# A two-layer decoder trunk in fp32 on one core: norms with 32 partitions per head, memory tiles ahead of the first query tile, and the inverses' recursion kept in program order

## The chip, the cores and the metric

The kernel runs on one core of one Trainium2 chip. The metric is the device time of one execution in microseconds. The engines are named as in the profile: PE is the matmul engine (PEld its weight loads), DVE the vector engine, ACT the scalar engine, POOL the GpSimd engine, SP the engine that issues most of the DMAs.

## The reference

One sequence of 256 tokens with 2048 channels passes through two layers. Each has one wide input projection, a token mixer, cross attention of four heads into 256 memory tokens, a gate silu(z), an output projection and a layer norm. The mixer of the first layer is a chunkwise retention, that of the second a gated delta rule. The change lies in the second layer:

```python
def gdn_branch(x, w_in, conv_w, a_log, dt_bias, norm_g):
    h = x @ w_in
    qkv = causal_conv_silu(h[..., :CONV_CH], conv_w)      # conv of width 4, then silu
    q = q * lax.rsqrt(jnp.sum(jnp.square(q), -1, keepdims=True) + NORM_EPS)
    k = k * lax.rsqrt(jnp.sum(jnp.square(k), -1, keepdims=True) + NORM_EPS)
    ...
    o = gated_delta_rule(q, k, v, g, beta)

def gated_delta_rule(q, k, v, g, beta):
    lower = jnp.where(strict, jnp.einsum('bhnid,bhnjd->bhnij', k_beta, kc) * decay, 0.0)
    a_mat = lower + jnp.eye(CHUNK, dtype=jnp.float32)
    u = lax.linalg.triangular_solve(a_mat, v_beta, left_side=True, lower=True, unit_diagonal=True)
    w = lax.linalg.triangular_solve(a_mat, k_beta * jnp.exp(g_cum)[..., None], left_side=True, lower=True, unit_diagonal=True)
    ...
```

There are 12 query and key heads of 128 channels and 24 value heads, so q and k are three tiles of four heads each (q0 to q2, k0 to k2).

## The kernel before, in words

**The weight stream.** All projections are split products: each fp32 weight is taken as a high and a low part, each activation too, and PE runs high by high, high by low and low by high. The weights come in units of 1024 numbers on each of 128 partitions (512 KB). SP issues a unit's DMA into one of four raw buffers; ACT rounds it to the high half (`split`, L173), DVE subtracts to get the low half (L174), and both go into rings of three. In the program's order a unit is loaded two units ahead of its use (`LOOK`). In the trace the units of the input projections are called `win_62` and the like, the halves `win_62h` and `win_62l`; for q, k and v tiles the matmuls with the high half are L303, those with the low half L310, and for z tiles both are L270.

**Order of the tiles.** `ORD1` lists the second layer's tiles: four tiles of the memory's keys and values (kv0 to kv3), the gates' columns (ab), the key tiles, the query tiles, two tiles of memory queries with their gates (mq, zm), and then the pairs v and z. The loop at the end of the function goes through this list; each tile's weights are streamed, and its result is handed to a generator.

**Work beside the stream.** The generators (`kq_tile`, `gdn_round`, `gdn_level`, `gdn_qc`, `gdn_pair` and others) are kept in `bg`. After every weight unit `bg.slot` lets them issue some work, by credits, in order of priority. So the stream is cut in many places by small groups of matmuls, and ACT, DVE and POOL run the generators' operations between the halves of the weights. The tile framework then settles the final order on each engine; an instruction in `tc.keep_in_program_order` stays behind everything that was traced before it on its engine.

**Norms of q and k** (`kq_tile`, L876 and following). After the conv (L864 to L871: an ACT copy, then three multiply-adds on DVE for each block of 128 channels, a tanh and a product) the squares of 128 channels have to be summed over the partitions. Two mults on POOL square the lower 64 partitions of two heads each (L886, 64x512), two ACT operations square the upper 64 (L887), POOL adds the two (L889, 128x512), and four matmuls (L895) with a selector of two columns sum over 64 partitions each.

**The inverses** (`gdn_gram`, `gdn_round`, `gdn_level`). The triangular matrices of four pairs of heads are inverted together: their blocks of 32 are copied to `LD` (L977, L979), transposed (L986), and a recursion of 31 steps on DVE, each a product (L993) and a subtraction (L995), gives the inverses of the blocks in `X`. Two transposes (L1002, L1004) follow, and `gdn_level` builds the inverses of 64 and 128 from them with small matmuls (named lv0 to lv5). `gdn_qc` makes the key and query products (`kq`, L1071 to L1073) and the weights `D` (L1078 to L1083).

Of the kernel before, what the change touches and what calls it, by code (L numbers as in the profile page):

```python
# [13 lines left out]
AF = mybir.ActivationFunctionType  # L14
ALU = mybir.AluOpType
AX = mybir.AxisListType

P = 128
# [20 lines left out]
PRM_NG, PRM_GG, PRM_CW, PRM_AL, PRM_DT, PRM_N = 0, 24, 25, 217, 218, 219  # L39
CST_ID, CST_U, CST_SU, CST_CAP, CST_IF, CST_SG, CST_SEL, CST_N = 0, 128, 256, 384, 512, 513, 514, 516  # L40

# [23 lines left out]
ORD0 = ["kv0", "kv1", "kv2", "kv3", "mq0", "zm0", "mq1", "zm1"]  # L65
ORD1 = ["kv0", "kv1", "kv2", "ab", "k0", "k1", "kv3", "q0", "mq0", "zm0", "mq1", "zm1", "k2", "q1", "q2"]
for _p in range(NPAIR):
# [59 lines left out]
def hybrid_kernel(ctx: ExitStack, tc: tile.TileContext, io: dict, stop=None):  # L127
    nc = tc.nc
# [11 lines left out]
    cst = cst_p.tile([P, CST_N], F32, name="cst")  # L140
# [4 lines left out]
    cap = cst[:, CST_CAP : CST_CAP + P]  # L145
    sel = cst[:, CST_SEL : CST_SEL + 2]
    mexp = cst_p.tile([P, 16], F32, name="mexp")
# [438 lines left out]
    for l, order, mem_ in ((0, ORD0, mem0), (1, ORD1, mem1)):  # L586
        j = 0
# [129 lines left out]
    for i, nm in enumerate(ORD0):  # L717
# [8 lines left out]
        p = int(nm[-1])  # L726
# [149 lines left out]
    def kq_tile(nm, ps):  # L876
        p = int(nm[1])
        lst, s0 = (kT, 8) if nm[0] == "k" else (qT, 9)
        lst[p] = stile(s0 + 2 * p, [P, 4, S], F32, nm + "T")
        src = lst[p]  # L880
        yield from conv(src, ps, (12 if nm[0] == "k" else 0) + 4 * p)
        fold = wtile("t2b", T2B, [P, 2, S], "fd" + nm)
        sq = wtile("t2", T2, [P, 2, S], "sq" + nm)
        for b in range(2):
            lo_, hi_ = src[0:64, 2 * b : 2 * b + 2, :], src[64:128, 2 * b : 2 * b + 2, :]
            nc.gpsimd.tensor_tensor(fold[64 * b : 64 * b + 64], lo_, lo_, op=ALU.mult)  # L886
            nc.scalar.activation(sq[64 * b : 64 * b + 64], hi_, AF.Square)  # L887
        yield 0.0
        nc.gpsimd.tensor_tensor(fold, fold, sq, op=ALU.add)  # L889
        yield 0.0  # L890
        yield 0.0
        pm = mx("n" + nm)
        for hh in range(2):
            for c in range(2):
                nc.tensor.matmul(pm[:, 4 * c + 2 * hh : 4 * c + 2 * hh + 2], fold[:, hh, c * P : c * P + P], sel, start=True, stop=True)  # L895
        hs = slice(4 * p, 4 * p + 4)
        pn = pm[:, 0:8].rearrange("p (c h b) -> p c b h", c=2, h=2)
        if nm[0] == "q":
# [63 lines left out]
    def gdn_round(rnd, wait, grams, s_ld, s_sl, s_x, wait2):  # L962
# [18 lines left out]
        SL = stile(s_sl, [P, 32, 32], F32, "SL%d" % rnd)  # L981
        X = stile(s_x, [P, 32, 32], F32, "X%d" % rnd)
# [7 lines left out]
        for j in range(31):  # L990
            n, m = 31 - j, j + 1
            t_ = tmp[:, 0 : n * m].rearrange("p (a b) -> p a b", b=m)
            nc.vector.tensor_tensor(t_, SL[:, j + 1 : 32, j : j + 1].broadcast_to([P, n, m]),  # L993
                                    X[:, j : j + 1, 0:m].broadcast_to([P, n, m]), op=ALU.mult)
            nc.vector.tensor_tensor(X[:, j + 1 : 32, 0:m], X[:, j + 1 : 32, 0:m], t_, op=ALU.subtract)  # L995
            acc += 2 * (n * m + 60) / 960.0
            if acc > 1.0:
                yield acc
                acc = 0.0
# [167 lines left out]
    for i, nm in enumerate(ORD1):  # L1167
# [3 lines left out]
        if nm == "ab":  # L1171
            bg.add(gates(ab_gemm()), 0)
            bg.slot()
            continue
        if nm == "q0":
            bg.add(gdn_round(0, kdone, [(0, 24), (1, 25), (2, 26), (3, 27)], 15, 19, 14, lambda: "pv11" in done), 3)
            for q in range(NPAIR):
                bg.add(gdn_level(q), 2)
                bg.add(gdn_qc(q), 2)
            bg.add(gdn_round(1, lambda p: QC[1] is not None, [(4, 8), (5, 9)], 15, 19, 26, lambda: Ts[3] is not None), 3)  # L1180
        ps = gemm(x1, 4, "l1" + nm, cm_tile(1, nm))
        p = int(nm[-1])
# [46 lines left out]
def layout(x, mem, positions, w_in_ret, ret_norm_g, w_in_gdn, conv_w, a_log, dt_bias, gdn_norm_g, w_mem_kv, w_out, ln_g, ln_b):  # L1229
# [33 lines left out]
    cst[:, CST_SG] = np.where(i < 64, 1.0, -1.0)  # L1263
    cst[:64, CST_SEL] = 1.0
    cst[64:, CST_SEL + 1] = 1.0
    io["cst"] = cst
# [29 lines left out]
```

## Time and profile before

| | |
|---|---|
| device time, median of 3 runs | 1665.41 us (1664.97 to 1665.59) |
| the profiled execution | 1667.04 us |
| its span, first to last instruction | 1665.3 us |
| PE busy | 1651.6 us (99%) |
| DVE busy | 1182.7 us (71%) |
| ACT busy | 827.9 us (50%) |
| POOL busy | 94.6 us (6%) |
| mean granted clock of PE | 0.997 |

An engine is busy while one of its instructions runs; idle time is put down to the instruction whose end released the next one. Records of neighbours on one engine can overlap by a little, so that what a group costs its engine is read from start to start. PEclk is the granted clock as a share of full speed: 1.00 stands for 2.4 GHz, 0.50 for 1.2 GHz.

### The profile page before, as it was taken

Reading aid. Unit: us, or ns where it says so; the run is one execution under the profiler, and the core shown is the slowest. Engines: PE = TensorE matmul, PEld = TensorE weight load, DVE = VectorE, ACT = ScalarE, POOL = GpSimd, SP = SyncE. Lnnn points to the kernel's source line nnn. Section 1 sums busy time; section 2 is a strip of 40 time slices with the busy share of each in tenths; the row PEclk is TensorE's granted clock in tenths of the full one; section 3 lists DMA queues with packets and bytes.
Section 4 is the critical chain, followed back from the end, with each engine's and each line's share of the span. In section 5 each row is a group of like instructions: output and inputs, shape, how many; then the busy total and the mean of one; then the engine's idle time right before and its main releaser. Section 6 shows DMA issues by size and latency. Waiting matters only on the chain.

```text
span 1665.3 us, 24140 instructions
## 1 busy us (share of the span) xinstructions
PE 1651.6 (99%) x9282; PEld 1420.9 (85%) x9282; DVE 1182.7 (71%) x1740; ACT 827.9 (50%) x1182; POOL 94.6 (6%) x101
## 2 busy tenths in 40 slices
PE   9999999999999999999999999999999999999997
PEld 8888888888888888888888888888888888888886
DVE  5666665877868776555879787699677999574556
ACT  5555544444444444344455565555556556454332
POOL 0000000000000000000001110012011012011000
PEclk9999999999999999999999999999999999999999
DMA  8765555656566575677665665555445555465663
GB/s 273 229 201 159 172 185 179 200 169 209 166 195 201 166 262 193 201 239 230 204 201 188 192 214 165 165 176 179 155 144 177 171 164 157 140 222 181 221 206 128
DMA packets 91171, 315.37 MB, mean 189 GB/s; under 512 B 10020, under 2 KB 11940, under 8 KB 91056
## 3 DMA queue, kind: packets, MB, share of 16 engines
q1 hardware_dynamic: 90448, 311.71, 58.0%
q0 software_dynamic: 608, 2.12, 0.4%
q8 instruction: 72, 1.18, 0.3%
q14 instruction: 43, 0.35, 0.1%
HBM read 309.58 MB, written 4.22 MB: 188 GB/s over the span
## 4 chain that ended last, share of the span: by engine, by line
PE 98%; DMA 1%; DVE 0%; issue 0%; ACT 0%; SPq 0%; DVEq 0%; ACTq 0%
PE wo L270 20%; PE l1z L270 8%; PE l0z L270 8%; PE l0v L270 8%; PE l1v L303 5%; PE l0qk L303 5%; PE kv L270 5%; PE l1v L310 3%; PE l0qk L310 3%; PE l1q L303 3%; PE l1k L303 3%; PE kv L303 3%; PE l1zm L303 2%; PE l0zm L303 2%; PE l1mq L303 2%; PE l0mq L303 2%
## 5 line engine op out<-in xcount | busy, mean ns | idle before, releaser
L457 DVE STREAM_TRANSPOSE br0tr<-ron 32x256 f32<-32x256 f32 x96 | 41.8, 436 | 2.0
L170 POOL TENSOR_TENSOR rc<-rc,mexp 128x4 f32<-128x4 f32 x6 | 6.1, 1010 | 586.1 <-DVE rc L695 586.1
L867 DVE SCALAR_TENSOR_TENSOR cv<-l1v_s,prm,cv 128x253 f32<-128x253 f32 (+2 forms) x72 | 32.5, 496 | 1.5 <-ACT cv L864 1.5
L995 DVE TENSOR_TENSOR X<-X,tmp 128x31 f32<-128x31 f32 (+15 forms) x62 | 23.6, 380 | 0.9
L993 DVE TENSOR_TENSOR tmp<-SL,X 128x31 f32<-128x31 f32 (+15 forms) x62 | 22.5, 362 | 0.7
L317 ACT ACTIVATE l1v_s<-l1v 128x512 f32<-128x512 f32 x12 | 7.2, 599 | 29.9 <-PE l1v L303 29.8
L170 POOL TENSOR_TENSOR lna<-lna,mexp 128x1 f32<-128x1 f32 x4 | 4.3, 1094 | 307.4 <-DVE lna L552 162.4
L952 DVE SCALAR_TENSOR_TENSOR dL<-gbcL,Gc,cst 128x128 f32<-128x128 f32 x48 | 15.8, 381 | 7.7 <-DMA gbcL<-GR 7.6
L1078 DVE SCALAR_TENSOR_TENSOR D<-gbcC,Gc,cst 128x128 f32<-128x128 f32 x48 | 15.7, 385 | 7.4 <-DMA gbcC<-GR 7.2
L499 DVE SCALAR_TENSOR_TENSOR r<-xr,wo 128x512 f32<-128x512 f32 x16 | 10.3, 683 | 14.5 <-PE wo L270 11.6
L1141 ACT ACTIVATE gsq<-go 128x128 f32<-128x128 f32 x48 | 12.6, 275 | 12.3 <-PE go L1134 10.1
L173 ACT ACTIVATE rsth<-dec 128x384 fp32r<-128x384 f32 x12 | 6.3, 526 | 24.5 <-DVE dec L667 24.5
L317 ACT ACTIVATE l0qk_s<-l0qk 128x512 f32<-128x512 f32 x12 | 7.2, 602 | 21.8 <-PE l0qk L303 21.8
L867 DVE SCALAR_TENSOR_TENSOR cv<-l1q_s,prm,cv 128x255 f32<-128x255 f32 (+2 forms) x36 | 17.6, 516 | 0.0
L867 DVE SCALAR_TENSOR_TENSOR cv<-l1k_s,prm,cv 128x255 f32<-128x255 f32 (+2 forms) x36 | 17.2, 511 | 0.0
L1015 POOL MEMSET T<- 128x1024 f32 x6 | 5.7, 952 | 202.2 <-PE w1p L1123 163.3
L954 ACT ACTIVATE dL<-dL 128x256 f32<-128x256 f32 x24 | 9.5, 415 | 14.8 <-DVE dL L952 14.4
L1081 ACT ACTIVATE D<-gbcC,suf 128x256 f32<-128x256 f32 x24 | 11.1, 503 | 10.8 <-DMA gbcC<-GR 8.9
L170 POOL TENSOR_TENSOR gc<-gc,mexp 128x8 f32<-128x8 f32 x6 | 10.1, 1683 | 104.0 <-DVE gc L1149 103.9
L705 DVE TENSOR_TENSOR ron<-ron,rz 128x1024 f32<-128x1024 f32 x6 | 7.4, 1225 | 12.0 <-ACT ron L703 12.0
L703 ACT ACTIVATE ron<-ro,rc 128x256 f32<-128x256 f32 x24 | 11.6, 564 | 8.2 <-DVE rc L697 8.2
L318 DVE TENSOR_TENSOR l0qk_s<-l0qk_s,l0qk 128x512 f32<-128x512 f32 x12 | 8.2, 683 | 10.2 <-ACT l0qk_s L317 10.2
(4207 smaller groups left out, 5479.9 us busy)
## 6 DMA issues: line engine op xcount, KB each, us to landing
win<-in_win_dram SPq DMA_DIRECT2D x352, 512.0 KB, 4.0
wout<-in_wout_dram SPq DMA_DIRECT2D x128, 512.0 KB, 4.3
wkv_kv<-in_wkv_dram SPq DMA_DIRECT2D x63, 512.0 KB, 4.2
gbcL<-GR SPq DMA_DIRECT2D x12, 256.0 KB, 3.7
gbcC<-GR SPq DMA_DIRECT2D x12, 256.0 KB, 3.7
dec<-in_dec_dram SPq DMA_DIRECT2D x12, 192.0 KB, 4.0
xr<-in_xT_dram SPq DMA_DIRECT2D x4, 512.0 KB, 3.9
lng<-in_lng_dram SPq DMA_DIRECT2D x4, 512.0 KB, 5.4
```

What stands on the lines that cost most here:

```text
L170: nc.gpsimd.tensor_tensor(out, in_, mexp[:, 0:n], op=ALU.pow)
L270: nc.tensor.matmul(outs[t], getattr(act, name)(g, kc0 + k2)[:, t * P : t * P + P], w_[:, k2, cs], **flags)
L303: nc.tensor.matmul(two[:, 512 * blk : 512 * blk + 512], wh[:, kc, blk * P : blk * P + P], flat(act.both(g, kc)), start=g == 0 and kc == 0, ...
L310: nc.tensor.matmul(two[:, 512 * blk : 512 * blk + S], wl[:, kc, blk * P : blk * P + P], act.hi(g, kc), start=False, stop=False, skip_group ...
L317: nc.scalar.activation(half(sm), parts[:, :, 1, :], AF.Copy)
L457: tc.keep_in_program_order(nc.vector.transpose(dst[o, ..., i], src[i, ..., o]))
L867: nc.vector.scalar_tensor_tensor(y[:, c, s_:], src[:, 0 : S - s_], cw(j), y[:, c, s_:], op0=ALU.mult, op1=ALU.add)
L952: nc.vector.scalar_tensor_tensor(dt[:, c, :], gbc[:, vl % 2, c * P : c * P + P], Gc[:, c, v : v + 1], cap, op0=ALU.subtract, op1=ALU.min)
L993: nc.vector.tensor_tensor(t_, SL[:, j + 1 : 32, j : j + 1].broadcast_to([P, n, m]), X[:, j : j + 1, 0:m].broadcast_to([P, n, m]), op=ALU.mult)
L995: nc.vector.tensor_tensor(X[:, j + 1 : 32, 0:m], X[:, j + 1 : 32, 0:m], t_, op=ALU.subtract)
L1078: nc.vector.scalar_tensor_tensor(d[:, 2 * c, :], gbc[:, vv, c * P : c * P + P], Gc[:, c, v : v + 1], cap, op0=ALU.subtract, op1=ALU.min)
L1141: nc.scalar.activation(sq[:, cs], o[:, cs], AF.Square, accum_out=cols[:, 4 * t + vl : 4 * t + vl + 1])
```

## The change

It has three parts, all in the second layer.

The norms use 32 partitions for each head. Each of the four quarters (32 partitions) of the four heads is squared by its own operation into the partitions of the head: two quarters on ACT (eight operations of 32x256), two on POOL (eight mults of 32x256). Two adds on POOL (128x512, 128x256) fold the four quarters into one, and two matmuls with a selector of four columns give the sums of all four heads. The selector in the constants grows from two columns to four.

In `ORD1` the tiles mq0, zm0, mq1 and zm1 stand ahead of q0 instead of behind it, and the generators of the inverses are handed in at mq0 instead of q0.

The 62 operations of a recursion are wrapped in `tc.keep_in_program_order`.

```diff
-ORD1 = ["kv0", "kv1", "kv2", "ab", "k0", "k1", "kv3", "q0", "mq0", "zm0", "mq1", "zm1", "k2", "q1", "q2"]
+ORD1 = ["kv0", "kv1", "kv2", "ab", "k0", "k1", "kv3", "mq0", "zm0", "mq1", "zm1", "q0", "k2", "q1", "q2"]
...
-    sel = cst[:, CST_SEL : CST_SEL + 2]
+    sel = cst[:, CST_SEL : CST_SEL + 4]
...
-        for b in range(2):
-            lo_, hi_ = src[0:64, 2 * b : 2 * b + 2, :], src[64:128, 2 * b : 2 * b + 2, :]
-            nc.gpsimd.tensor_tensor(fold[64 * b : 64 * b + 64], lo_, lo_, op=ALU.mult)
-            nc.scalar.activation(sq[64 * b : 64 * b + 64], hi_, AF.Square)
-        yield 0.0
+        for q in range(4):
+            for h in range(4):
+                from_, to = src[32 * q : 32 * q + 32, h, :], slice(32 * h, 32 * h + 32)
+                if q < 2:
+                    nc.scalar.activation(fold[to, q, :], from_, AF.Square)
+                else:
+                    nc.gpsimd.tensor_tensor(sq[to, q - 2, :], from_, from_, op=ALU.mult)
+            yield 0.0
         nc.gpsimd.tensor_tensor(fold, fold, sq, op=ALU.add)
+        nc.gpsimd.tensor_tensor(fold[:, 0, :], fold[:, 0, :], fold[:, 1, :], op=ALU.add)
         yield 0.0
         yield 0.0
         pm = mx("n" + nm)
-        for hh in range(2):
-            for c in range(2):
-                nc.tensor.matmul(pm[:, 4 * c + 2 * hh : 4 * c + 2 * hh + 2], fold[:, hh, c * P : c * P + P], sel, start=True, stop=True)
+        for c in range(2):
+            nc.tensor.matmul(pm[:, 4 * c : 4 * c + 4], fold[:, 0, c * P : c * P + P], sel, start=True, stop=True)
...
-            nc.vector.tensor_tensor(t_, SL[:, j + 1 : 32, j : j + 1].broadcast_to([P, n, m]),
-                                    X[:, j : j + 1, 0:m].broadcast_to([P, n, m]), op=ALU.mult)
-            nc.vector.tensor_tensor(X[:, j + 1 : 32, 0:m], X[:, j + 1 : 32, 0:m], t_, op=ALU.subtract)
+            tc.keep_in_program_order(nc.vector.tensor_tensor(t_, SL[:, j + 1 : 32, j : j + 1].broadcast_to([P, n, m]),
+                                                             X[:, j : j + 1, 0:m].broadcast_to([P, n, m]), op=ALU.mult))
+            tc.keep_in_program_order(nc.vector.tensor_tensor(X[:, j + 1 : 32, 0:m], X[:, j + 1 : 32, 0:m], t_, op=ALU.subtract))
...
-        if nm == "q0":
+        if nm == "mq0":
             bg.add(gdn_round(0, kdone, [(0, 24), (1, 25), (2, 26), (3, 27)], 15, 19, 14, lambda: "pv11" in done), 3)
```

Lines behind L889 of the kernel before have a number three higher in the changed one (L993 and L995 become L996 and L998, L1055 becomes L1058).

On PE, around the last level matmuls of the first two pairs of heads (lv0t, lv1t) and the norm matmuls of q2 (nq). Before:

```order
L303 MATMUL l1v_0_10656<-x1b_6704,win_96h 128x512 x2
L1055 MATMUL lv0t_10395<-T_10148,lv0y2n 64x64 x8
L1055 MATMUL lv1t_10405<-T_10171,lv1y2n 64x64 x8
L895 MATMUL nq_10437<-cst,fdq_10264 128x2 x4
L303 MATMUL l1v_0_10656<-x1b_6704,win_96h 128x512 x2
```

After:

```order
L270 MATMUL l1z_10506<-win_92h,x1a_6707 128x512 x6
L1058 MATMUL lv0t_10431<-T_10143,lv0y2n 64x64 x8
L1058 MATMUL lv1t_10441<-T_10166,lv1y2n 64x64 x8
L270 MATMUL l1z_10506<-win_92h,x1a_6707 128x512 x2
L270 MATMUL l1z_10506<-win_92l,x1a_6707 128x512 x4
L270 MATMUL l1z_10506<-win_93h,x1b_6708 128x512 x8
L270 MATMUL l1z_10506<-win_93l,x1b_6708 128x512 x4
L270 MATMUL l1z_10506<-win_94h,x1a_6709 128x512 x8
L898 MATMUL nq_10575<-cst,fdq_10377 128x4 x2
L270 MATMUL l1z_10506<-win_94l,x1a_6709 128x512 x4
```

The norm matmuls of q2 stood right behind the two levels and now stand 26 wide matmuls of the stream behind them.

On DVE, the start of the recursion (SL is the transposed input, X the inverse being built, `win_..l` low halves of weights, cv the conv). Before:

```order
L174 TENSOR_TENSOR win_62l<-win_62_9446,win_62h 128x1024
L986 STREAM_TRANSPOSE SL_9497<-LD_9380 128x1024
L867 SCALAR_TENSOR_TENSOR cv_0_9582<-l1k_s_9442,prm,cv_0_9582 128x255 x2
L431 TENSOR_TENSOR ma_3os<-ma_3os,zm_9308 128x512
L993 TENSOR_TENSOR tmp_9546<-SL_9497,X_9498 128x31
L174 TENSOR_TENSOR win_63l<-win_63_9473,win_63h 128x1024
L867 SCALAR_TENSOR_TENSOR cv_0_9582<-l1k_s_9442,prm,cv_0_9582 128x254 x2
L995 TENSOR_TENSOR X_9498<-X_9498,tmp_9546 128x31
L174 TENSOR_TENSOR br1b_9408<-ma_3os,br1b_9408 128x2x256
```

After:

```order
L174 TENSOR_TENSOR win_54l<-win_54_9211,win_54h 128x1024
L989 STREAM_TRANSPOSE SL_9262<-LD_9145 128x1024
L867 SCALAR_TENSOR_TENSOR cv_0_9347<-l1q_s_9207,prm,cv_0_9347 128x255 x2
L431 TENSOR_TENSOR ma_3os<-ma_3os,zm_9073 128x512
L174 TENSOR_TENSOR win_55l<-win_55_9238,win_55h 128x1024
L867 SCALAR_TENSOR_TENSOR cv_0_9347<-l1q_s_9207,prm,cv_0_9347 128x254 x2
L174 TENSOR_TENSOR br1b_9173<-ma_3os,br1b_9173 128x2x256
L867 SCALAR_TENSOR_TENSOR cv_0_9347<-l1q_s_9207,prm,cv_0_9347 128x253
L174 TENSOR_TENSOR win_56l<-win_56_9266,win_56h 128x1024
L867 SCALAR_TENSOR_TENSOR cv_0_9347<-l1q_s_9207,prm,cv_0_9347 128x253
L174 TENSOR_TENSOR win_57l<-win_57_9289,win_57h 128x1024
L996 TENSOR_TENSOR tmp_9311<-SL_9262,X_9263 128x31
```

The recursion now begins eight weight units earlier in the stream, beside the conv of q0 instead of k2, and its first step stands behind three more low halves. From win_54l to win_87l, where it now ends, DVE's order holds 33 low halves, 48 conv operations L867 and four products D; from win_62l to win_91l before it held 29, 36 and none.

On POOL, the norms beside the recursion (fdk, fdq, sqk, sqq hold the squares; NK is a power of the key norms). Before:

```order
L886 TENSOR_TENSOR fdk_9736<-k2T 64x512 x2
L889 TENSOR_TENSOR fdk_9736<-fdk_9736,sqk_9737 128x512
L886 TENSOR_TENSOR fdq_9957<-q1T 64x512
L909 TENSOR_TENSOR NK<-nk_9830,mexp 128x2x4
L886 TENSOR_TENSOR fdq_9957<-q1T 64x512
L889 TENSOR_TENSOR fdq_9957<-fdq_9957,sqq_9958 128x512
```

After:

```order
L890 TENSOR_TENSOR sqq_9502<-q0T 32x256 x8
L892 TENSOR_TENSOR fdq_9501<-fdq_9501,sqq_9502 128x512
L893 TENSOR_TENSOR fdq_9501<-fdq_9501 128x256
L890 TENSOR_TENSOR sqk_9761<-k2T 32x256 x8
L892 TENSOR_TENSOR fdk_9760<-fdk_9760,sqk_9761 128x512
L893 TENSOR_TENSOR fdk_9760<-fdk_9760 128x256
L890 TENSOR_TENSOR sqq_10009<-q1T 32x256 x4
L912 TENSOR_TENSOR NK<-nk_9968,mexp 128x2x4
L890 TENSOR_TENSOR sqq_10009<-q1T 32x256 x4
```

Three POOL operations of a tile have become ten, and the tiles beside the recursion are now q0, k2 and q1; those of q2 stand behind the copies that wait for the finished inverses.

## Rows read from the trace of the kernel before

**Rows 1.** The first part of the profile's page: busy time of each engine, its share of the span and its instructions.

```profile
PE 1651.6 (99%) x9282; PEld 1420.9 (85%) x9282; DVE 1182.7 (71%) x1740; ACT 827.9 (50%) x1182; POOL 94.6 (6%) x101
```

**Rows 2.** The view of waits for PE, the first and the last of its five rows: engine and line, what it waited for, us in total, times, longest.

```profile
PE warmps L167 <- DVE warm L164: 1.2, 1, 1.2
...
PE kv L289 <- DVE wkv_kv04l L174: 0.2, 1, 0.2
```

**Rows 3.** Windows: us, then busy time (and instructions) of PE, PEld, DVE, ACT and POOL, the granted clock of PE, the DMA engines' busy share, GB/s.

```profile
1080.00:1120.00 40.00, 40.00 (x235) 35.30 (x234) 39.83 (x75) 23.10 (x31) 4.61 (x4) 1.00 0.55 173
...
1188.80:1192.20 3.40, 3.40 (x13) 3.02 (x12) 3.40 (x9) 1.06 (x1) 0.00 (x0) 0.50 0.00 0
...
1078.86:1166.32 87.46, 87.46 (x499) 76.79 (x498) 86.88 (x153) 49.44 (x68) 17.41 (x13) 1.00 0.55 175
```

**Rows 4.** Timelines of DVE and PE: when the low halves of win_62 and win_91 were made, and when PE first used them. Columns: start, us, engine, line, operation, output and inputs, count.

```profile
1077.63 1.23 DVE L174 TENSOR_TENSOR win_62l<-win,win_62h 128x1024 fp32r<-128x1024 f32 x1 [0.26 <-ACT win_62h L173]
...
1084.59 0.64 PE L310 MATMUL l1k<-x1a,win_62l 128*128 128x256 f32 x4
...
1165.13 1.19 DVE L174 TENSOR_TENSOR win_91l<-win,win_91h 128x1024 fp32r<-128x1024 f32 x1
...
1168.51 0.86 PE L270 MATMUL l1z<-win_91l,x1b 128*128 128x512 f32 x3
```

**Rows 5.** Timeline of PE around the norm matmuls of a key tile.

```profile
922.66 0.95 PE L895 MATMUL nk<-cst,fdk 128*128 128x2 f32 x8
923.47 0.96 PE L270 MATMUL kv<-wkv_kv34h,mem1a 128*128 128x512 f32 x3
```

**Rows 6.** Timeline of PE around the levels of the first two pairs of heads.

```profile
1178.83 0.69 PE L1048 MATMUL lv0y<-lv0x,L 64*64 64x64 f32 x9
...
1180.38 0.97 PE L270 MATMUL l1z<-win_94l,x1a 128*128 128x512 f32 x3
...
1185.36 1.14 PE L1055 MATMUL lv0t<-T,lv0y2n 64*64 64x64 f32 x16
...
1187.37 1.05 PE L895 MATMUL nq<-cst,fdq 128*128 128x2 f32 x8
1188.28 0.77 PE L303 MATMUL l1v<-x1b,win_96h 128*128 128x512 f32 x2
...
1189.70 1.06 PE L310 MATMUL l1v<-x1b,win_96l 128*128 128x256 f32 x4
1190.55 1.85 PE L303 MATMUL l1v<-x1a,win_97h 128*128 128x512 f32 x4
1192.24 1.09 PE L303 MATMUL l1v<-x1b,win_97h 128*128 128x512 f32 x4
1193.17 0.63 PE L310 MATMUL l1v<-x1a,win_97l 128*128 128x256 f32 x4
1193.64 0.64 PE L310 MATMUL l1v<-x1b,win_97l 128*128 128x256 f32 x4
```

**Rows 7.** POOL's groups by line and shape in the window 1078.86 to 1166.32 (busy us, mean ns, idle before and its releaser), and under them four of DVE's instructions from the timeline of that window.

```profile
L889 POOL TENSOR_TENSOR fdq<-fdq,sqq 128x512 f32<-128x512 f32 x2 | 3.3, 1666 | 1.9 <-ACT sqq L887 1.8
L886 POOL TENSOR_TENSOR fdq<-q1T 64x512 f32<-64x512 f32 x2 | 2.9, 1462 | 13.5 <-DVE q1T L871 13.4
L886 POOL TENSOR_TENSOR fdq<-q2T 64x512 f32<-64x512 f32 x2 | 2.3, 1132 | 16.3 <-DVE q2T L871 16.3
L886 POOL TENSOR_TENSOR fdk<-k2T 64x512 f32<-64x512 f32 x2 | 2.1, 1052 | 33.7 <-DVE k2T L871 33.7
L889 POOL TENSOR_TENSOR fdk<-fdk,sqk 128x512 f32<-128x512 f32 x1 | 1.3, 1296 | 0.1
...
1102.27 0.36 DVE L995 TENSOR_TENSOR X<-X,tmp 128x192 f32<-128x192 f32 x1
...
1126.91 1.26 DVE L867 SCALAR_TENSOR_TENSOR cv<-l1q_s,prm,cv 128x255 f32<-128x255 f32 x1
1128.09 2.31 DVE L174 TENSOR_TENSOR win_79l<-win,win_79h 128x1024 fp32r<-128x1024 f32 x1
...
1150.90 1.46 DVE L995 TENSOR_TENSOR X<-X,tmp 128x192 f32<-128x192 f32 x1
```

**Rows 8.** Groups of instructions by line and shape (busy us, mean ns, idle before), of POOL and ACT and then of DVE, and two rows of PE's timeline at the products of q0 and k0.

```profile
L979 POOL COPY LD<-L 32x256 f32<-32x256 f32 x12 | 4.7, 391 | 50.6 <-PE ma_3s L372 50.2
L148 POOL MEMSET mexp<- 128x8 f32 x1 | 0.1, 104 | 0.3 <-POOLq L1292 0.3
L977 ACT ACTIVATE LD<-L 32x256 f32<-32x256 f32 x12 | 5.0, 415 | 0.9 <-PE ma_3s L372 0.7
...
L867 DVE SCALAR_TENSOR_TENSOR cv<-l1q_s,prm,cv 128x253 f32<-128x253 f32 x8 | 3.7, 470 | 0.0
L871 DVE SCALAR_TENSOR_TENSOR q1T<-q1T,cv 128x512 f32<-128x512 f32 x2 | 1.4, 678 | 0.0
L318 DVE TENSOR_TENSOR l1q_s<-l1q_s,l1q 128x512 f32<-128x512 f32 x4 | 2.7, 676 | 0.0
L1083 DVE TENSOR_TENSOR D<-kq,D 128x512 f32<-128x512 f32 x18 | 11.8, 682 | 1.3 <-PE kq L1073 1.1
...
982.94 0.68 PE L1071 MATMUL kq<-q0T,k0T 128*128 128x256 f32 x2
...
983.82 1.17 PE L303 MATMUL l1zm<-x1a,win_32h 128*128 128x512 f32 x4
```

More of the change, by code (lines that the diff above doesn't have):

```diff
@@ L39 @@
 PRM_NG, PRM_GG, PRM_CW, PRM_AL, PRM_DT, PRM_N = 0, 24, 25, 217, 218, 219
-CST_ID, CST_U, CST_SU, CST_CAP, CST_IF, CST_SG, CST_SEL, CST_N = 0, 128, 256, 384, 512, 513, 514, 516
+CST_ID, CST_U, CST_SU, CST_CAP, CST_IF, CST_SG, CST_SEL, CST_N = 0, 128, 256, 384, 512, 513, 514, 518
 def in_tiles(base_v, base_mq, base_z, first):
@@ L892, in kq_tile @@
         pm = mx("n" + nm)
-        for hh in range(2):
-            for c in range(2):
-                nc.tensor.matmul(pm[:, 4 * c + 2 * hh : 4 * c + 2 * hh + 2], fold[:, hh, c * P : c * P + P], sel, start=True, stop=True)
+        for c in range(2):
+            nc.tensor.matmul(pm[:, 4 * c : 4 * c + 4], fold[:, 0, c * P : c * P + P], sel, start=True, stop=True)
         hs = slice(4 * p, 4 * p + 4)
-        pn = pm[:, 0:8].rearrange("p (c h b) -> p c b h", c=2, h=2)
+        pn = pm[:, 0:8].rearrange("p (c b h) -> p c b h", c=2, b=2)
         if nm[0] == "q":
@@ L1263, in layout @@
     cst[:, CST_SG] = np.where(i < 64, 1.0, -1.0)
-    cst[:64, CST_SEL] = 1.0
-    cst[64:, CST_SEL + 1] = 1.0
+    for h in range(4):
+        cst[32 * h : 32 * h + 32, CST_SEL + h] = 1.0
     io["cst"] = cst
```

## The prediction, made before the changed kernel had run

> **What bounds the kernel now.** I read the page's busy times first: PE, the matmul engine, is busy for 1651.6 of 1665.3 us and the next engine, DVE, for 1182.7 [rows 1]. Then the waits of PE: there are five, from 1.2 down to 0.2 us and 3.4 together, all on the warm-up tile, the first weights and the first activations [rows 2]. So in the second layer, where the whole change lies, PE never waits. Its time can move in three ways only: PE gets less or more work, its granted clock differs, or a wait that isn't there now comes up. A saving on any other engine is worth nothing by itself.
>
> The windows show where a wait could come up. While the recursion for the triangular inverses runs, DVE is as full as PE: 39.83 busy of the 40.00 us from 1080 to 1120, and 86.88 of the 87.46 us from 1078.86 to 1166.32, whereas ACT has 38 us idle in that stretch and POOL 70 [rows 3]. The timelines show how near it is. Every weight unit needs its low half from DVE (L174) before PE can run the last part of that unit. That of win_62 is done at 1078.86 and first used at 1084.59, 5.73 us later; that of win_91 is done at 1166.32 and used at 1168.51, 2.19 us later [rows 4]. Over those 29 units DVE falls behind PE by 3.5 us and has 2.2 left. The same windows show one dip of the clock, 0.50 from 1188.80 to 1192.20.
>
> **The norm matmuls: -2.2 us.** Before, each of the six query and key tiles sums its squares with four matmuls of two columns, and each leaves two records. Eight records run from 922.66 to 923.47, 0.81 us, with the last of them overlapping what follows; a record costs about 0.11 [rows 5]. Afterwards there are two matmuls of four columns, four records. No row shows four columns, but a record of 64 columns takes (1187.37 - 1185.36)/32 = 0.06 [rows 6], so four are hardly dearer than two: 6 tiles x 4 records fewer, at 0.06 to 0.11, are -1.5 to -2.6 us. I take -2.6, since these are records of the same instruction. Against that, the wide stream is cut in about four more places (the order of PE puts the two norm matmuls of q0 apart, and other small groups fall elsewhere); a cut costs about 0.1 us, the overlap that the neighbours lose, so +0.4.
>
> **The clock dip: -1.5 us.** Four L310 start 0.85 us apart as a group at 1189.70 and four L303 take 1.69 at 1190.55; at full clock such groups take 0.47 (1193.17 to 1193.64) and 0.93 (1192.24 to 1193.17). Eight L310 and four L303 fell into the dip: 2 x (0.85 - 0.47) + (1.69 - 0.93) = 1.5 us lost [rows 6]. What came ahead of it is one run of small matmuls from 1185.36 to 1188.28: 32 records of 64x64 for the levels of two pairs of heads (lv0t and lv1t, the first 16 shown) and eight norm records of q2 right behind them, 2.9 us without a wide matmul. A run of small ones from 1178.83 to 1180.38, 1.55 us, was not followed by a dip [rows 6]. The order shows q2's norm matmuls 26 wide ones behind the levels after the change, so this run gets shorter by its norm part. I take the dip as gone. If it stays, or another comes, the term is 0.
>
> The Trainium skill (TensorE: Matmul & The Clock Gate, section Why this matters for your kernels) ties drops in the middle of a kernel to idle gaps of PE between bursts of matmuls. This trace does not agree here: PE is busy 3.40 of 3.40 us in the dip and its five waits are all at the start [rows 2, 3]. By that rule the reordering would leave the dip as it is, and the sum would be 1665.7.
>
> **DVE's debt in the recursion: +2.5 us.** This is the term that decides. I compare the recursion's stretch in both orders. Before it runs beside 29 weight units (win_63 to win_91), after beside 33 (win_55 to win_87), since q0 now falls into it too.
> PE's side: 1168.51 - 1084.59 = 83.9 us before [rows 4]. Added: four units, each 8 x 0.23 + 8 x 0.12 = 2.8, so 11.2 [rows 6]; the six matmuls of two heads' key-query products, twice 983.82 - 982.94 = 0.88, so 1.8 [rows 8]; and 8 norm records fewer, -0.9. After: 96.0.
> DVE's own work: it is 86.88 less what it loses to POOL. Nine DVE operations of this stretch are stretched, each just while POOL runs one of its nine tensor operations of the norms (L886, L889): L867 takes 1.26 at 1126.91 where 0.47 is usual, win_79l 2.31 where 1.2 is usual, L995 of 128x192 1.46 where 0.36 is usual [rows 4, 7, 8]. The losses are 0.11 in one case and 0.7 to 1.1 in the others, 7.1 together. So DVE's own work is 79.8. Added in the changed stretch, by the counts of the order: four low halves at 1.15 (a record overlaps the next by some 0.08, as at 1126.91 and 1128.09), 4.6; twelve L867 at 0.39, 4.7; two L871 and one L318 at 0.60 each, 1.8; four products D at 0.60, 2.4 [rows 8]. After: 93.3.
> Losses to POOL: before, the nine POOL operations take 3.3 + 2.9 + 2.3 + 2.1 + 1.3 = 11.9 us and DVE loses 7.1; with 0.25 taken off each operation the rows give 3 x (2 x 0.78 + 1.04) = 7.8, of which 7.1 is 0.9 [rows 7]. After the change a tile has eight mults of 32x256, one add of 128x512 and one of 128x256 on POOL. No row has a 32x256 mult. Below stands the copy of that shape, 0.39; above, the mult of 64x512, 1.03. The smallest POOL operation takes 0.10 [rows 7, 8], so half the elements make (1.03 - 0.10)/2 + 0.10 = 0.57, which I take: nearer to the copy, but with two inputs as the mult. The 128x256 add comes out likewise at 0.70. A tile then costs DVE 8 x 0.32 + 1.04 + 0.45 = 4.05, three tiles (q0, k2, q1; q2's come behind the inverses) 12.2, times 0.9 = 10.9.
> Balance: 5.7 us of lead at the start, if the first low half of the stretch is as early as before, + 96.0 - 93.3 = +2.7, - 10.9: the low half is 2.5 us late at the end, and PE waits for it in pieces, the first waits of the second layer. The pin lets low halves traced before a recursion step go ahead of it on DVE, but it takes no work off DVE; as long as DVE is the later one, the order of its work only moves these waits.
> By price: at 0.39 the loss is 7.0 and there is no wait; at 1.03 it is 20.9 and the wait is 12.4.
>
> The Trainium skill (SBUF — State Buffer, section Who interferes with whom) says that a DVE instruction with two SBUF inputs contends with a GpSimd instruction that reads SBUF, and that whoever comes first holds the shared pair for its whole instruction while the other is blocked. The trace agrees that only such pairs stretch, and the loss of 7.1 in 11.9 us shows less than whole durations. Whole durations are the slower rival below.
>
> **Edits that I cost at nothing.** ACT gets eight squares of 32x256 a tile, 8 x 0.415 = 3.3 us, three tiles 10 us [rows 8]: ACT's 38 idle us hide them. If they queued ahead of a high half, PE would wait for that; the largest such wait would be one tile's 3.3. The memory tiles moved ahead of q0 are the same number of units, so SP issues as many DMAs, in another order; DMA's share of 0.55 in the stretch leaves room [rows 3]. q2's matmuls wait for POOL's eight mults and two adds behind the inverses, 8 x 0.57 + 1.3 + 0.7 = 6.5 us; by the order some 18 us of PE work stand in between. Behind such a late matmul the whole of PE would queue, but here only after 11 us more.
>
> **Sum.** -2.2 - 1.5 + 2.5 = -1.2 us. The profiled run took 1667.04 us, 1.7 more than its span and 1.6 more than the median of the runs, 1665.41; I take the difference off the median: 1664.2.
>
> **Rivals.**
> No wait: the mults cost near the copy's 0.39, or DVE finds cover that I don't count. Then -3.7: 1661.7. For it: POOL's copies of just this shape. Against: two inputs.
> Slower: POOL blocks DVE for whole instructions or its small mults are dear. Whole durations give 3 x (8 x 0.57 + 1.29 + 0.70) = 19.7 us lost, a wait of 11.2, so +7.5: 1672.9. It decides from a mult of 0.63 (loss 12.1, wait 3.7, no gain left), and is measurably slower from 0.78. For it: a mult that waits for DVE in its turn stretches too (L886 of q1 took 1.46 on average against 1.05 for k2) [rows 7], and eight short ones one behind the other give DVE more collisions. Against: 7.1 lost of 11.9.
> The dip stays, since small matmuls are not its cause, or the new waits bring another: no -1.5, so 1665.7. For it: one instance only. Against: nothing else of that length lies ahead of it.
> That the change does not do what it says is little likely: the order shows all three parts.
>
> **Chances.** Forecast 0.50, no wait 0.22, slower 0.15, dip stays 0.13. The forecast's own range follows from mults of 0.48 to 0.70: waits of 0.5 to 5.3, so 1662.3 to 1667.0. The range leaves out the far half of the two outer cases: 1661.0 to 1669.5. Some 0.2%, 3.3 us, is what a measurement of this kernel tells from no change: below 1662.1 lie most of the no-wait case and a little of the forecast, 0.24; above 1668.7 the slower case and a little more, 0.17; between, 0.59.
>
> **What would show it.** Waits of PE on L174's low halves, 2 to 3 us in total, near the end of the recursion's stretch and nowhere else; mults of 32x256 at about 0.57; 24 norm records instead of 48; clock 1.00 throughout the levels of the first heads. No waits with mults of 0.4 would show the first rival; over 7 us of waits and DVE operations of 2 us, the second; a stretch at 0.50, the third. Waits on ACT's high halves or on q2's sums would show that I missed a queue.

## The result, and the profile after

The changed kernel took 1677.08 us (median of four runs, 1674.06 to 1677.63) beside 1665.23 us for the kernel before: 1.0067 times as long, 95% interval 1.0055 to 1.0078. The forecast of 1664.2 us was wrong in sign, and the time lies above its range.

The execution that was profiled is the fastest of the four, 1674.06 us with a span of 1672.3; so its trace explains 7.0 us of span. What the others have more is read from a second trace and from their mean clocks (below). First the page's busy times, as in [rows 1]:

```profile
PE 1652.8 (99%) x9258; PEld 1418.7 (85%) x9258; DVE 1187.8 (71%) x1740; ACT 837.6 (50%) x1218; POOL 134.1 (8%) x143
```

PE has 24 records fewer, as worked out, and POOL 39.5 us more busy time, part of which will turn out to be waiting for DVE. PE's waits in the window from 1050 to 1200, where [rows 2] had none (engine and line, what it waited for, us in total, times, longest):

```profile
PE nq L898 <- POOL fdq L893: 3.3, 1, 3.3
PE lv1tb L1043 <- DVE EQ L903: 1.0, 1, 1.0
PE lv0ya L1023 <- DVE X L1007: 0.8, 1, 0.8
PE l1v L310 <- DVE win_81l L174: 0.7, 1, 0.7
PE l1v L310 <- DVE win_80l L174: 0.3, 1, 0.3
```

These are 6.1 us. The last two are the late low halves that the prediction spoke of, and the third is DVE's lateness in another place, the inverses. The second is a PSUM bank that is free when DVE has read q1's sums from it (EQ); DVE is not full there, but EQ stands in its queue behind the low half of win_90, which waits 0.26 us for ACT's high half. The first, the largest, is the sum of q2's squares, which I had put at nothing. Windows, as in [rows 3] (us, busy time and instructions of PE, PEld, DVE, ACT and POOL, granted clock, DMA share, GB/s): the recursion's stretch from the low half of win_54 to that of win_87, and a stretch in which PE's granted clock falls to half, called a dip from here on.

```profile
1052.58:1157.29 104.71, 102.96 (x645) 89.36 (x645) 103.77 (x177) 66.05 (x106) 31.35 (x34) 1.00 0.52 166
...
1189.56:1192.97 3.41, 3.41 (x9) 2.63 (x8) 1.65 (x2) 0.53 (x1) 0.00 (x0) 0.50 0.39 117
```

DVE is busy for 103.77 of 104.71 us. Its own work was put at 93.3, so it lost some 10.5 us to POOL; the forecast was 10.9. Taken one by one, 24 DVE operations of the stretch, all beside POOL's norms, take 10.5 us more than such operations usually do. The groups of POOL's mults in the same stretch (busy us, mean ns, idle before):

```profile
L890 POOL TENSOR_TENSOR sqq<-q1T 32x256 f32<-32x256 f32 x8 | 8.1, 1015 | 8.3 <-DVE q1T L871 7.9
L890 POOL TENSOR_TENSOR sqk<-k2T 32x256 f32<-32x256 f32 x8 | 7.5, 937 | 17.0 <-DVE k2T L871 11.2 <-ACT win_70h L173 5.4
L890 POOL TENSOR_TENSOR sqq<-q0T 32x256 f32<-32x256 f32 x8 | 5.0, 622 | 33.4 <-DVE q0T L871 33.1
```

Beside q0 a mult takes 0.62 us, near the 0.57 of the estimate. Beside k2 and q1 the means are 0.94 and 1.02: five of those sixteen mults, each begun while DVE was at a low half, took 1.10 to 2.01 us, the other eleven 0.61 to 0.80. So POOL waits for DVE as DVE does for POOL. The timeline of DVE at the last four mults of q1, which POOL runs from 1129.79 to 1133.10, is the other side of it (start, us, instruction, count):

```profile
1129.21 1.21 DVE L174 TENSOR_TENSOR win_79l<-win,win_79h 128x1024 fp32r<-128x1024 f32 x1
1130.35 1.58 DVE L867 SCALAR_TENSOR_TENSOR cv<-l1q_s,prm,cv 128x254 f32<-128x254 f32 x2
1131.85 0.78 DVE L996 TENSOR_TENSOR tmp<-SL,X 128x207 f32<-128x207 f32 x1
1132.56 1.63 DVE L174 TENSOR_TENSOR win_80l<-win,win_80h 128x1024 fp32r<-128x1024 f32 x1
```

Two L867 take 1.58 where two take 0.86 elsewhere (at 1184.80, below), a low half 1.63 instead of 1.21, and win_80l is one of the two that PE waits for.

The late sum of q2 is another story. POOL's timeline, then DVE's, then PE's, at the end of the levels of the first two pairs:

```profile
1171.62 7.32 POOL L890 TENSOR_TENSOR sqq<-q2T 32x256 f32<-32x256 f32 x8 [10.72 <-PE lv1y L1051]
1179.02 7.78 POOL L892 TENSOR_TENSOR fdq<-fdq,sqq 128x512 f32<-128x512 f32 x1
1186.87 0.72 POOL L893 TENSOR_TENSOR fdq<-fdq 128x256 f32<-128x256 f32 x1
```

```profile
1178.99 2.44 DVE L867 SCALAR_TENSOR_TENSOR cv<-l1v_s,prm,cv 128x255 f32<-128x255 f32 x6
1181.35 1.21 DVE L174 TENSOR_TENSOR win_95l<-win,win_95h 128x1024 fp32r<-128x1024 f32 x1
1182.48 1.26 DVE L867 SCALAR_TENSOR_TENSOR cv<-l1v_s,prm,cv 128x254 f32<-128x254 f32 x3
1183.67 1.21 DVE L174 TENSOR_TENSOR win_96l<-win,win_96h 128x1024 fp32r<-128x1024 f32 x1
1184.80 0.86 DVE L867 SCALAR_TENSOR_TENSOR cv<-l1v_s,prm,cv 128x253 f32<-128x253 f32 x2
```

```profile
1182.39 1.98 PE L270 MATMUL l1z<-win_94h,x1a 128*128 128x512 f32 x8
1187.65 0.61 PE L898 MATMUL nq<-cst,fdq 128*128 128x4 f32 x4 [3.28 <-POOL fdq L893]
```

POOL's mults do not begin behind the inverses, at 1161, but at 1171.62, released by PE's lv1y: their target `sq` takes one of three buffers that conv and levels share. They take 7.32 us. The add that follows begins at 1179.02, 0.03 us after DVE has begun a run of thirteen instructions without a gap; that run ends at 1185.66, and the add 1.1 us later, at 1186.80. An add otherwise takes 1.3; with such an add the sum would have been ready at about 1181.0 (an estimate: the mults' end at 1178.94, and 1.3 and 0.7), ahead of PE, which comes to the norm matmul at 1184.37. As it is, PE, whose queue has the norm matmul next, stands for 3.28 us, and two microseconds later its clock falls to 0.50 for 3.41 us.

### The profile page after: what moved, and what is told of

It is laid out like the page before. It is cut to its first block, busy times and chain, and to the rows that moved or that the text cites. A ratio compares the mean times of both kernels' runs of the same rounds, so it can differ in the third digit from the quotient of the medians.

```text
span 1672.3 us, 24172 instructions
## 1 busy us (share of the span) xinstructions
PE 1652.8 (99%) x9258; PEld 1418.7 (85%) x9258; DVE 1187.8 (71%) x1740; ACT 837.6 (50%) x1218; POOL 134.1 (8%) x143
## 5 line engine op out<-in xcount | busy, mean ns | idle before, releaser
L867 DVE SCALAR_TENSOR_TENSOR cv<-l1v_s,prm,cv 128x255 f32<-128x255 f32 (+2 forms) x72 | 33.9, 518 | 0.9 <-ACT cv L864 0.9
L996 DVE TENSOR_TENSOR tmp<-SL,X 128x31 f32<-128x31 f32 (+15 forms) x62 | 23.0, 372 | 0.6
L998 DVE TENSOR_TENSOR X<-X,tmp 128x31 f32<-128x31 f32 (+15 forms) x62 | 22.5, 363 | 0.8
L867 DVE SCALAR_TENSOR_TENSOR cv<-l1q_s,prm,cv 128x255 f32<-128x255 f32 (+2 forms) x36 | 20.0, 582 | 0.0
L867 DVE SCALAR_TENSOR_TENSOR cv<-l1k_s,prm,cv 128x255 f32<-128x255 f32 (+2 forms) x36 | 17.9, 529 | 0.0
```

The lines of the kernel that those rows point to most:

```text
L867: nc.vector.scalar_tensor_tensor(y[:, c, s_:], src[:, 0 : S - s_], cw(j), y[:, c, s_:], op0=ALU.mult, op1=ALU.add)
L996: tc.keep_in_program_order(nc.vector.tensor_tensor(t_, SL[:, j + 1 : 32, j : j + 1].broadcast_to([P, n, m]), X[:, j : j + 1, 0:m].broadcas ...
L998: tc.keep_in_program_order(nc.vector.tensor_tensor(X[:, j + 1 : 32, 0:m], X[:, j + 1 : 32, 0:m], t_, op=ALU.subtract))
```

## The experiments

Thirteen runs, two of them of a kernel without an edit, each beside fresh runs of the kernel before (medians 1665.2 to 1665.5 us), ratios with their 95% interval.

**The changed kernel once more (after_again).** No edit.

> The changed kernel once more, unchanged, to see how far its executions differ among themselves (the profiled one took 1674.06 us, three others 1676.7 to 1677.6). Theory A (the norms' POOL work is late: q2's sum reaches PE 3.4 us late, the inverses 3 us late, and PE's clock falls behind such a wait): about 1674 or 1677 us, and where the time is nearer 1677 the trace shows one more stretch at a granted clock of 0.50 than the first trace, which had one of 3.4 us. Rival B (the executions differ by the waits themselves): no further stretch at 0.50, but waits of PE above the 6.1 us of the second layer in the first trace.

1675.26 us, 1.0056 (1.0044 to 1.0069); the profiled execution 1675.72, span 1674.0. The same waits, 6.1 us, and two stretches at half clock, the first behind the waits at the levels:

```profile
1163.99:1167.40 3.41, 3.41 (x27) 2.77 (x25) 3.22 (x7) 0.00 (x0) 0.00 (x0) 0.50 0.73 220
1191.29:1194.70 3.41, 3.41 (x10) 2.64 (x9) 1.60 (x2) 0.64 (x1) 0.00 (x0) 0.50 0.38 118
```

Its span is 1.7 us above that of the first trace; 0.1 of it lies in the first 21 us, 1.5 in the additional dip. Theory A holds for the two traces. The executions without a trace agree: the record lists the mean granted clock of each, and one dip of 3.41 us takes 0.001 off it. Of the changed kernel's nine executions the one at 0.998 took 1672.30 us, those at 0.997 and 0.996 took 1674.06 to 1675.72, and those at 0.995 1676.48 to 1677.63. So the median of the first four, 1677.08, is that of executions with some three such dips (an estimate from these means).

**The norms alone (norms_only) and undone (norms_undone).** The first is the kernel before with the new `kq_tile` and selector, the second the changed kernel with the old ones.

> The kernel before with the new norms alone; order of tiles and recursion as before. Theory A (the new norms' mults on POOL make DVE and PE late, wherever the tiles stand): slower than before by 3 to 10 us, with waits of PE on low halves or on the inverses between 1120 and 1170 and on POOL's sum of q2. Rival C (the reordered tiles and the pin do it, the norms save their 24 records): 1662 to 1664 us, no waits of PE in the second layer.

> The changed order and the pinned recursion with the norms of the kernel before. Theory A: within 2 us of the kernel before (1663 to 1667 us), PE without waits of more than 1 us in the second layer. Rival C: most of the 12 us stays, 1672 us or more, with waits of PE on low halves between 1120 and 1170.

norms_only: 1672.08 us, 1.0038 (1.0024 to 1.0052). As slow as Theory A had it, but the places differ: PE waits 2.7 us at gvp for DVE's product gv (L871), 1.3 us for win_38l, 0.6 for win_83l and 0.5 for win_145l. norms_undone: 1668.01 us, 1.0015 (1.0006 to 1.0024), with 0.4 us of wait at lv0ya. That is 1 us above what Theory A allowed and far below Rival C. So order and pin cost 2.6 us without the new norms, and the new norms some 7 to 9 us more. Norms_only's trace also has a dip, from 1372.03, at the end of the wait at gvp (the transposes of gv on PE).

**All squares on ACT (act_squares).**

```diff
-                if q < 2:
-                    nc.scalar.activation(fold[to, q, :], from_, AF.Square)
-                else:
-                    nc.gpsimd.tensor_tensor(sq[to, q - 2, :], from_, from_, op=ALU.mult)
+                nc.scalar.activation((fold if q < 2 else sq)[to, q % 2, :], from_, AF.Square)
```

> The changed kernel with all sixteen squares of a tile on ACT; POOL keeps the two adds. Theory A (POOL's mults are what delays DVE and the sum of q2): 1662 to 1666 us; PE's waits on low halves, on the inverses and on POOL's sum of q2 are gone or under 1 us together. Rival D (it is the adds, or the late start of q2's squares, whichever engine makes them): the wait on q2's sum stays at 2 us or more, and the time above 1668 us. If ACT becomes late instead, PE waits on high halves (L173), which the trace would name.

1665.12 us, 0.9998 (0.9988 to 1.0007). All waits of the second layer are gone, and no stretch stands at half clock ahead of the last microseconds, where every trace has one. Theory A: moving eight mults a tile off POOL takes back 10 to 12 us. Rival D falls: the adds are as they were. The norms without POOL's mults are worth 1665.12 - 1668.01 = -2.9 us.

**The mults replaced by memsets (memset_mults).** What remains to be told apart is POOL's time and its reads. This kernel leaves out half of the squares.

```diff
-                    nc.gpsimd.tensor_tensor(sq[to, q - 2, :], from_, from_, op=ALU.mult)
+                    nc.gpsimd.memset(sq[to, q - 2, :], 0.25)
+                    nc.gpsimd.memset(sq[to, q - 2, :], 0.5)
```

> The changed kernel with each of POOL's mults of 32x256 replaced by two memsets of the same tile (0.30 us each, so about the 0.61 us of an undisturbed mult); the sums then hold a constant in place of half the squares, so the outputs differ from the reference's. Theory A (the mults cost by delaying DVE's operations that read two SBUF operands): 1664 to 1667 us, no stretched DVE operations beside the memsets, PE's waits on low halves and inverses under 1 us together. Rival I (what costs is POOL's time and queue, whatever it runs): 1671 us or more, with the waits of the changed kernel.

1665.30 us, 0.9998 (0.9989 to 1.0008), no waits in the second layer. POOL's and DVE's timelines at the memsets of k2:

```profile
1078.21 2.46 POOL L890 MEMSET sqk<- 32x256 f32 x7
1080.72 0.30 POOL L891 MEMSET sqk<- 32x256 f32 x1
```

```profile
1079.57 1.21 DVE L174 TENSOR_TENSOR win_63l<-win,win_63h 128x1024 fp32r<-128x1024 f32 x1
1080.71 0.47 DVE L867 SCALAR_TENSOR_TENSOR cv<-l1k_s,prm,cv 128x255 f32<-128x255 f32 x1
```

POOL is as busy as with undisturbed mults, and the DVE operations beside it take their usual 1.21 and 0.47. So it is not POOL's time but its reading beside DVE's that costs. Rival I falls. One thing differs besides: a memset has no input to wait for, so those of q0 begin at 1056.71 instead of 1062.34; those of q2 wait for lv1y as the mults did.

**Half the mults (half_mults).** Three quarters of each tile on ACT, one on POOL (`if q < 3` ahead of the ACT form).

> The changed kernel with four of a tile's eight POOL mults moved to ACT (three quarters on ACT, one on POOL). Theory A (a debt against slack: DVE first uses up its lead of some 8 us and only what is above it costs PE time; POOL's sum of q2 comes before DVE's run of back-to-back operations): three tiles lose 3 x 4 x 0.4 = 5 us less on DVE, so the waits on low halves and on q2's sum go, 1665 to 1667 us. Rival L (each mult costs its share): half of the 10 us between act_squares (1665.1 us) and the changed kernel stays, 1669.5 to 1671 us.

1665.88 us, 1.0001 (0.9992 to 1.0010), no waits. Half the mults cost 0.8 us more than none, and the two intervals overlap; the other half cost 9 to 11. So there is no price per mult, and Rival L falls. With Theory A the low halves have a lead that is used up first, and q2's add, at 1172.91 here, comes ahead of DVE's long run and takes 1.29 us.

**The buffer of its own (own_sq).**

```diff
-        sq = wtile("t2", T2, [P, 2, S], "sq" + nm)
+        sq = wtile("t2n", 1, [P, 2, S], "sq" + nm)
```

> The changed kernel, but the second buffer of squares (sq) has a ring of its own instead of one slot of the three that the conv and the levels use. POOL's squares of q2 then no longer wait for a level's matmuls and stand ahead of the levels' copies. Theory A: the wait of 3.3 us on POOL's sum of q2 is gone, but a fourth tile's mults fall into the recursion, so that DVE is later: waits on low halves and on the inverses rise from 3.1 to between 5 and 8 us; 1672 to 1677 us in all. Rival H (the late sum of q2 is the main loss, and the recursion has room): 1668 to 1671 us, waits on low halves and inverses stay at 3 to 4 us.

1670.68 us, 1.0033 (1.0021 to 1.0045). PE's waits of the second layer now:

```profile
PE lv0ya L1023 <- DVE X L1007: 1.9, 1, 1.9
...
PE l1v L310 <- DVE win_81l L174: 0.7, 1, 0.7
PE l1v L303 <- ACT win_86h L173: 0.6, 1, 0.6
...
PE l1v L310 <- DVE win_80l L174: 0.3, 1, 0.3
```

The 3.3 us are gone, and with the fourth tile in the recursion PE waits 1.1 us longer for the inverses; behind that wait the trace has a dip, from 1160.67. Rival H holds in its time, and nearly in its waits (2.9 us for low halves and inverses); of Theory A's payback only the 1.1 us and 0.6 on a high half came. The gain is 4.6 us against after_again.

**Order and pin apart (order_only, pin_only, unpinned).** order_only is the kernel before with the new `ORD1` and the generators at mq0; pin_only the kernel before with the pinned recursion; unpinned the changed kernel without the pin.

> The new order of tiles alone: old norms, recursion not pinned. With order and pin the time was 1668.0 us. Theory F (the order itself costs, by the places at which it cuts the wide stream and by the inverses that come a little late for PE): 1667 to 1669 us, the same waits as with the pin. Rival G (the pin costs, since steps of the recursion wait behind low halves): 1665 to 1666 us, and lv0ya without a wait.

> The kernel before with the pinned recursion alone. The pin went with 1.7 us in two pairs (1668.0 against 1666.3 us with old norms, 1665.1 against 1663.5 us with squares on ACT), both in the new order, and in both without a wait of PE above 0.4 us. Theory P (the pin itself costs, since the inverses come later and PE's small matmuls stand elsewhere): 1667 us, slower than before by 1.2 to 2 us. Rival Q (it costs in the new order alone, by where that order lets the levels fall): 1665.4 us, within 0.6 us of before.

> The changed kernel with the recursion not pinned, mults on POOL as in the change. Theory A (DVE as a whole is late, the pin only says for whom): low halves wait more and the inverses less than with the pin, the sum of PE's waits in the second layer within 1.5 us of the changed kernel's 6.1, the time 1673 to 1677 us. Rival K (the pin makes the waits): waits under 4 us, 1671 us or less.

order_only: 1666.28 us, 1.0006 (0.9998 to 1.0015); its interval still holds no change, and Rival G comes nearer than Theory F. pin_only: 1666.79 us, 1.0011 (1.0002 to 1.0020): the pin costs some 1.6 us by itself (Theory P), with no wait of PE that the view names; where PE loses them is not settled. unpinned: 1669.24 us, 1.0026 (1.0017 to 1.0035), waits of 2.6 us. Rival K was right on the time and on the sum, but not in its reason: low halves and inverses wait as with the pin (0.9 and 0.7 us, lv1tb 1.0), but q2's sum is no longer late:

```profile
1173.81 7.29 POOL L890 TENSOR_TENSOR sqq<-q2T 32x256 f32<-32x256 f32 x8 [12.85 <-PE lv1y L1051]
1181.18 1.35 POOL L892 TENSOR_TENSOR fdq<-fdq,sqq 128x512 f32<-128x512 f32 x1
1182.62 0.80 POOL L893 TENSOR_TENSOR fdq<-fdq 128x256 f32<-128x256 f32 x1
```

The mults take as long and end as late after lv1y, but the add begins before DVE's long run, which starts at 1181.91, and takes 1.35 us instead of 7.78. DVE's order is not the same there; that the pin shifts the two against each other was seen, not aimed at.

**The kernel before once more (before_again).** No edit.

> The kernel before once more, for its trace. Theory M (the stretch at a granted clock of 0.50 that the first trace showed at 1188.80 comes in some executions only, and that trace was of one of them, 1667.04 us against a median of 1665.41): a time of 1665 to 1666 us and no stretch at 0.50 before the end. Rival N (the dip is in every execution, and what makes 1.6 us of difference is elsewhere): the dip of 3.4 us at about 1188.8 again, in a time of 1665 to 1666 us.

1665.12 us, 0.9997 (0.9987 to 1.0007); the profiled execution took 1666.37 with a span of 1664.6. The window of [rows 3] in which the first trace has 0.50:

```profile
1188.80:1192.20 3.40, 3.40 (x22) 3.06 (x22) 3.40 (x9) 1.91 (x3) 0.00 (x0) 1.00 0.11 46
```

The levels and q2's norms stand there as in [rows 6], in one run from 1186.22 to 1189.14, and the clock stays at 1.00. Two rows of PE's timeline, which [rows 6] have at 1187.37 and 1193.17:

```profile
1188.22 1.05 PE L895 MATMUL nq<-cst,fdq 128*128 128x2 f32 x8
...
1192.47 0.64 PE L310 MATMUL l1v<-x1a,win_97l 128*128 128x256 f32 x4
```

The same matmuls take 5.80 us with the dip and 4.25 without it, so it costs 1.55. This profiled execution is nevertheless 1.25 us above its median. Part of that lies at the first weights: at 20.99 us it is 0.87 us behind the first trace. The dip comes in some executions only, and the typical one has none: of the 93 fresh runs of the kernel before, 75 have a mean granted clock of 0.998 and times up to 1666.3, 18 have 0.997 and, but for one, 1666.0 to 1667.7.

**Squares on ACT in the old order, and without the pin (act_old_order, act_unpinned).**

> The new norms with all sixteen squares on ACT, in the tile order and with the unpinned recursion of the kernel before. Theory A (the norms' fewer PE records are worth 2.6 us, POOL's mults take it and more away, the new order costs some 2.6 us by itself): 1665.4 - 2.6 = 1662.8 us, 1662 to 1664, and no waits of PE in the second layer. Rival E (the gain of putting the squares on ACT belongs to the new order, which needs it; in the old order ACT delays high halves): 1665 us or more, with waits of PE on high halves (L173) or on ACT's squares.

> The changed kernel with all sixteen squares on ACT and the recursion not pinned. Theory A with order_only's result (new order 1666.3 us, norms' records -2.6 us where POOL makes no squares): 1663.7 us, 1663 to 1664.5, faster than the kernel before by 1 to 2 us. Rival J (the fewer norm records give nothing here, the pin is not what act_squares lost to): 1665 us as act_squares.

act_old_order: 1670.36 us, 1.0028 (1.0016 to 1.0039). Neither theory: the time is in Rival E's range, but ACT is not late, and still PE waits, for DVE's gv. PE's timeline:

```profile
1370.61 0.66 PE L1101 MATMUL gvp<-cst,gv 128*128 128x128 f32 x4 [2.40 <-DVE gv L871]
```

norms_only has the same wait of 2.4 us at the same instruction. With the new norms in the old order the scheduler puts that product late on DVE: behind the low half of win_149, where the kernel before has it behind that of win_147, while PE's products stand ahead of win_148 in both. This part of norms_only's loss comes neither from POOL's mults nor from the norms' work.

act_unpinned: 1663.46 us, 0.9987 (0.9978 to 0.9996). No waits in the second layer. This is the one version that beats both kernels, by 2 and by 12 to 14 us. With these two runs the price of POOL's mults can be read three times: 1.7 us in the old order (norms_only less act_old_order, with overlapping ranges), 5.8 in the new order without the pin (unpinned less act_unpinned), and 10 to 12 with both. It depends on where they fall.

## Why the prediction was wrong

**The norm matmuls, -2.2.** Right: -2.9 (act_squares against norms_undone) and -2.8 (act_unpinned against order_only); PE's busy time falls by 2.2 us in both pairs of traces.

**The clock dip, -1.5.** Wrong twice. The step "I take the difference off the median" and the term -1.5 counted one thing two times: the profiled execution of before was 1.6 us above the median, of which the dip is 1.55, and the typical execution has none (before_again). Its price of 1.5 was right, but against the median the term is 0. And the changed kernel has one or two dips in its traces, behind the new waits, at 1.5 us each, and by the mean clocks some three in its median execution. Of the rivals, "the new waits bring another" came true in these traces.

**DVE's debt, +2.5.** Right in mechanism and near in size. Losses were 10.5 us against 10.9, mults 0.62 against 0.57, and PE's waits in the stretch to 1157 are 0.3 + 0.7 + 0.8 = 1.8 us. The 1.0 at lv1tb behind it is of another kind, EQ's place in DVE's queue. memset_mults and half_mults show the mechanism; own_sq shows that with one more tile in the stretch PE waits 1.1 us longer for the inverses.

**q2's sum, 0.** This is the step that failed most clearly: the largest wait comes from it, the one of which the prediction says that it "would show that I missed a queue". The step "8 x 0.57 + 1.3 + 0.7 = 6.5 us; by the order some 18 us of PE work stand in between" had two faults. The start was taken from POOL's order, where the copies stand ahead, and not from what the target buffer waits for: lv1y, some ten microseconds later. And the 6.5 us took POOL alone, though the same text had DVE stretched by POOL and its slower rival named a POOL mult that "waits for DVE in its turn": the three steps took 16.0 us (1171.62 to 1187.6). The late start alone would not have made PE wait: the mults start as late in unpinned, where the add takes 1.35 us and the sum is ready at 1183.42, 3 us before PE comes to it. The add's 7.78 us decided. Wait and dip behind it make 4.8 us; own_sq, which removes them, is 4.6 us below after_again although PE waits longer for the inverses there.

**Order and pin, 0.** Costed at nothing, measured +1.0 (not certain) and +1.6. That the pin "takes no work off DVE" was true and not the point. What PE loses by them is not shown.

The sum against the median by what the runs show: -2.9 + 1.0 + 1.6 + 6.1 of waits + 1.5 or 3.1 of dips = 7.3 or 8.9, so 1672.7 or 1674.3. The traces' executions were 1674.06 and 1675.72: 1.4 us are left in both, and their cause stays open. Without a dip the sum is 1671.2, and the execution at a mean clock of 0.998 took 1672.30. The median of the first four, 1677.1, lies above its trace by further dips, as the mean clocks say. The slower rival named a kindred mechanism, "POOL blocks DVE", and 1672.9 us, but for the wrong reason: it made low halves wait 11 us, and the wait that came was POOL's own.

## What to carry to other kernels

When two engines slow each other, work out the loss on both sides: here DVE's loss was sized to half a microsecond and POOL's own delay, on which PE waited, was left at its undisturbed price. The start of a moved step is read from what its output buffer waits for, not from its place in the queue alone. And before an event of one profiled execution (a dip of the clock) becomes a term, see whether the median execution has it: here the mean clocks of the executions without a trace and a second trace said so. The distance from the median alone does not, since the second trace stood 1.25 us above its median without a dip.

## What the runs showed of the hardware

A POOL add of 128x512, 1.3 us by itself, took 7.78 us in both traces of the changed kernel, when it began just behind the start of thirteen DVE operations without a gap, and ended 1.1 us after the last of them. The Trainium skill (SBUF — State Buffer, section Who interferes with whom) says that whoever issues first holds the shared pair for the whole instruction; here the one that came second did not get it between instructions either, over 6.7 us. Of DVE's thirteen, each of the conv's takes two SBUF operands, as does a low half. That is not so everywhere: in the same trace, with DVE without a gap too, a mult of k2 that began within the low half of win_67 ran right behind it, and DVE's next L867 was the one that waited, 0.83 us instead of 0.47. POOL's row, then DVE's:

```profile
1090.43 1.46 POOL L890 TENSOR_TENSOR sqk<-k2T 32x256 f32<-32x256 f32 x1 [11.21 <-DVE k2T L871]
```

```profile
1090.21 1.21 DVE L174 TENSOR_TENSOR win_67l<-win,win_67h 128x1024 fp32r<-128x1024 f32 x1
1091.35 0.83 DVE L867 SCALAR_TENSOR_TENSOR cv<-l1k_s,prm,cv 128x255 f32<-128x255 f32 x1
```

What decides whether POOL gets in between two DVE operations is not shown.

Dips of the granted clock to 0.50 lasted 3.41 us and cost about 1.5 us each in these traces; unpinned has one of 6.83 us. In the traces with POOL's mults they began at the end of a wait of PE of 1.0 to 3.3 us or some 2 us behind it. Such a wait does not always bring one: the first trace of the changed kernel has none behind the 1.0 us at lv1tb, where the second has one, and act_old_order has none behind its 2.40 us. In one of two traces of the kernel before a dip came behind a run of small matmuls without any wait; the other trace of that kernel, with the same run, has none there.
